# Two DMA queues, one for loads and one for stores, and uniform six-row chunks in a softmax with a relative-position bias

## The chip, the cores and the metric

The kernel runs on one core of a Trainium2 chip. The metric is device time in microseconds for one launch, the median of three runs. The work below is done by VectorE (DVE), ScalarE (ACT) and the 16 DMA engines; SyncE (SP) issues transfers, GpSimd (POOL) makes a few index numbers at the start, and TensorE isn't used.

## The reference

```
B, H, S = 2, 8, 2112          # logits (B, H, S, S) f32, rel_bias (H, 33) f32
rel  = pos[:, None] - pos[None, :]
bias = rel_bias[:, clip(rel, -16, 16) + 16]      # (H, S, S)
x = logits + bias
out = exp(x - x.max(-1)) / sum(exp(x - x.max(-1)))
```

Each of the 2 x 8 x 2112 = 33,792 rows of 2,112 numbers (8,448 bytes) gets a bias that depends on the column's distance from the diagonal alone, and then a softmax. The input and the output are 285.47 MB each.

## The kernel before

**Layout.** A partition holds W = 33 neighbouring rows of one head, so 64 partitions hold a head (64 x 33 = 2112) and 128 partitions hold two. A loop over K = 4 pairs of heads contains the two batch entries; each is cut into chunks of 6, 5, 6, 5, 6 and 5 rows a partition (SIZES). A round has NT = 12 chunks, and the whole kernel 48. Four buffers X (NBUF = 4) of 6 rows each take the chunks in turn.

**The bias.** Within one head, a partition's rows differ only in where the bias band lies. For every pair of heads, strip(k) (lines 143 to 158) builds one strip F of 2112 + 32 columns in SBUF, and row i of a chunk adds a window of F that starts one column further left per row. The masks eq, lt and gt of the strip lie in PSUM (Z). The bias table is fetched once by a DMA that ACT issues (line 107), and spread over partitions by a shuffle on DVE (line 134).

**A chunk's chain.** Line numbers are those of the profile.
- load (line 88): one DMA on SP's queue; 128 partitions, each a contiguous run of 5 or 6 rows.
- add on DVE (line 173): for each row one custom instruction, x + bias in place with the row's negated maximum as a by-product; semaphore `added`.
- exps on ACT (line 181): for each row exp in place, with the row's sum as a by-product; semaphore `expd`.
- scale on DVE: a reciprocal over the chunk's sums (line 189) once all rows are through, and the first DV = 3 rows multiplied by it (line 193). scale_rest on ACT: the other 2 or 3 rows (line 198). DVE and ACT take all this in program order, so the adds of a chunk come behind the scalings of the chunk before.
- store (line 96): one DMA, also on SP's queue, once the rows are scaled.

Waits on a semaphore are recorded under line 83, the helper take.

**SP's order.** SP is the only engine that issues these transfers, in an order written out by hand (turn, lines 210 to 214): store chunk n; wait until the store of chunk n-1 has landed; load chunk n+3 into the buffer that this has freed. Loads and stores so alternate in one queue. The last chunk is stored in two parts.

Of the kernel before, what the change touches and what calls it, by code (L numbers as in the profile page):

```python
# [15 lines left out]
def kernel(  # L16
# [14 lines left out]
    assert NB * W == S and 2 * NB == P and H % 2 == 0  # L31
    FW = S + W - 1
    BIG = 3.0e38
    NBUF = 4
    SIZES = [6, 5, 6, 5, 6, 5]
    R = max(SIZES)
    assert sum(SIZES) == W

    CH = [(b, sum(SIZES[:i]), r) for b in range(B) for i, r in enumerate(SIZES)]
    NT = len(CH)  # L40
    assert NT % NBUF == 0
# [4 lines left out]
    rbP = io.tile([P, H // 2, W], FP32, tag="rbP", name="rbP")  # L46
    rbK = io.tile([P, W], FP32, tag="rbK", name="rbK")
    rest = io.tile([P, NB], FP32, tag="rest", name="rest")
    nmax = io.tile([P, NBUF * R], FP32, tag="nmax", name="nmax")
    tot = io.tile([P, NBUF * R], FP32, tag="tot", name="tot")  # L50
    rec = io.tile([P, NBUF * R], FP32, tag="rec", name="rec")
    ps = ctx.enter_context(tc.tile_pool(name="ps", bufs=1, space=bass.MemoryType.PSUM))
    Z = ps.tile([P, 512], FP32, tag="Z", name="Z")
    eq, lt, gt = (Z[:, i * NB : (i + 1) * NB] for i in range(3))

    def view(t, offset, dims):
        return bass.AP(tensor=t.tensor, offset=t.offset + offset, ap=[[list(t.ap[0])[0], P]] + dims)

    def rows(t, k, m, s0, n):

        b, j, r = CH[m]
        return bass.AP(
            tensor=t.tensor,
            offset=t.offset + (b * H * S + j + s0) * S + k * (2 * S * S),
            ap=[[W * S, P], [1, n * S]],
        )

    with tc.tile_critical(no_gpsimd_drain=True):  # L68
# [5 lines left out]
        scaledA = nc.alloc_semaphore("scaledA")  # L74
        inv = nc.alloc_semaphore("inv")
        invA = nc.alloc_semaphore("invA")
# [5 lines left out]
        def take(eng, sem, n):  # L82
            eng.wait_ge(sem, n).then_inc(sem, -n)  # L83


        def load(k, m):
            b, r = m % NBUF, CH[m][2]
            nc.sync.dma_start(out=X[b][:, 0 : r * S], in_=rows(logits, k, m, 0, r)).then_inc(ld[b], 16)

        def store(k, m, s0=0, n=None):  # L90
            b, n = m % NBUF, n or CH[m][2]
# [4 lines left out]
            nc.sync.dma_start(  # L96
                out=rows(out, k, m, s0, n), in_=X[b][:, s0 * S : (s0 + n) * S]
            ).then_inc(st[b], 16)

        for m in range(NBUF):  # L100
            load(0, m)

        Q = 32
        step = list(F.ap[0])[0]
        nc.vector.memset(F[:, 0 : H * W], 0.0).then_inc(zero, 1)  # L105
        nc.scalar.wait_ge(zero, 1)
        nc.scalar.dma_start(
            out=bass.AP(tensor=F.tensor, offset=F.offset, ap=[[Q * step, P // Q], [1, H * W]]),
            in_=bass.AP(tensor=rel_bias.tensor, offset=rel_bias.offset, ap=[[0, P // Q], [1, H * W]]),
        ).then_inc(rb, 16)  # L110
        for p0 in (0, NB):
            nc.gpsimd.iota(  # L112
                F[p0 : p0 + NB, H * W : H * W + NB], pattern=[[-1, NB]], base=0,
                channel_multiplier=1, allow_small_or_imprecise_dtypes=True,
            ).then_inc(idx, 1)

        v = nc.vector
        done = [0]
# [11 lines left out]
        iq = F[:, H * W : H * W + NB]  # L130
        for m, op in ((eq, ALU.is_equal), (lt, ALU.is_gt), (gt, ALU.is_lt)):
            then(v.tensor_scalar(out=m, in0=iq, scalar1=0.0, scalar2=None, op0=op))  # L132
        v.wait_ge(rb, 16)
        then(v.stream_shuffle(out=F[:, 0 : H * W], in_=F[:, 0 : H * W], mask=[0] * Q))  # L134
        settle()
        for h in range(2):
            p = slice(h * NB, (h + 1) * NB)
            src = bass.AP(tensor=F.tensor, offset=F[p].offset + h * W,
                          ap=[[list(F.ap[0])[0], NB], [2 * W, K], [1, W]])
            then(v.tensor_copy(out=rbP[p], in_=src))  # L140
        settle()

        def strip(k):

            then(v.tensor_copy(out=rbK[:, :], in_=rbP[:, bass.ds(k, 1), :]))  # L145
            settle()
            low, high = rbK[:, W - 1 : W], rbK[:, 0:1]
            blocks = view(F, MR, [[W, NB], [1, W]])
            then(v.tensor_tensor(out=blocks, in0=view(eq, 0, [[1, NB], [0, W]]),  # L149
                                 in1=view(rbK, W - 1, [[0, NB], [-1, W]]), op=ALU.mult))  # L150
            then(v.tensor_scalar(out=rest, in0=lt, scalar1=low, scalar2=None, op0=ALU.mult))  # L151
            then(v.tensor_copy(out=F[:, 0:MR], in_=low.to_broadcast([P, MR])))  # L152
            then(v.tensor_copy(out=F[:, FW - MR : FW], in_=high.to_broadcast([P, MR])))  # L153
            settle()
            then(v.scalar_tensor_tensor(out=rest, in0=gt, scalar=high, in1=rest, op0=ALU.mult, op1=ALU.add))  # L155
            settle()
            then(v.tensor_tensor(out=blocks, in0=blocks, in1=view(rest, 0, [[1, NB], [0, W]]), op=ALU.add))  # L157
            settle()

        def row(m, i):  # L160
            return X[m % NBUF][:, i * S : (i + 1) * S]

        def col(t, m, i, n=1):
            c = m % NBUF * R + i
            return t[:, c : c + n]

        DV = 3

        def add(m):
            take(v, ld[m % NBUF], 16)  # L170
            j, r = CH[m][1:]
            for i in range(r):
                v.tensor_tensor_reduce(  # L173
                    out=row(m, i), in0=row(m, i), in1=F[:, W - 1 - j - i : W - 1 - j - i + S],
                    scale=-1.0, scalar=BIG, op0=ALU.add, op1=ALU.min, accum_out=col(nmax, m, i),
                ).then_inc(added, 1)

        def exps(m):
            for i in range(CH[m][2]):
                take(nc.scalar, added, 1)  # L180
                nc.scalar.activation(  # L181
                    out=row(m, i), in_=row(m, i), func=ACTF.Exp, scale=-1.0, bias=col(nmax, m, i),
                    accum_out=col(tot, m, i),
                ).then_inc(expd, 1)

        def scale(m):
            r = CH[m][2]
            take(v, expd, r)
            v.reciprocal(out=col(rec, m, 0, r), in_=col(tot, m, 0, r)).then_inc(inv, 1)  # L189
            v.wait_ge(inv, 1).then_inc(inv, -1)  # L190
            v.sem_inc(invA, 1)
            for i in range(DV):
                v.tensor_scalar_mul(out=row(m, i), in0=row(m, i), scalar1=col(rec, m, i)).then_inc(scaled, 1)  # L193

        def scale_rest(m):
            take(nc.scalar, invA, 1)
            for i in range(DV, CH[m][2]):
                nc.scalar.activation(  # L198
                    out=row(m, i), in_=row(m, i), func=ACTF.Copy, scale=col(rec, m, i),
                ).then_inc(scaledA, 1)  # L200
# [19 lines left out]
        store(0, 0)  # L220
        with nc.Fori(0, K - 1, 1, engines=[ENG.SP]) as k:
            turn(k, 1, NT + 1)
        turn(K - 1, 1, NT - 3)
        for m in range(NT - 3, NT - 1):
            store(K - 1, m)
        r = CH[NT - 1][2]
        store(K - 1, NT - 1, 0, DV)
        store(K - 1, NT - 1, DV, r - DV)
        for b in range(NBUF):
            take(nc.sync, st[b], 32 if b == (NT - 1) % NBUF else 16)  # L230


# [28 lines left out]
```

## Time and profile before

| | |
|---|---|
| median of 3 runs | 1330.0 us (1329.25 to 1330.1) |
| profiled execution | 1329.3 us, span 1327.5 us |
| DVE, ACT busy | 819.7 us, 808.8 us |
| add, 264 rows, mean of one | 2354 ns (and 82 ns to read the maximum) |
| exp, 264 rows, mean of one | 2054 ns (and 187 ns to read the sum) |
| scaling, DVE 144 rows, ACT 120 rows, mean of one | 1316 ns, 2046 ns |
| DMA | 13,981 packets, 571.00 MB, mean 430 GB/s |
| load, store of 6 rows, issue to landing (median) | 39.7 us, 46.9 us |

The span runs from the first to the last recorded event on the core; the execution's own time is 1.8 us longer. The time from issue to landing includes the wait behind other transfers in the queue. In the tables of the profile each row is a line of the kernel, an engine and an operation, with its count, total and mean time.

### The profile page before, as it was taken

Reading aid. Unit: us, or ns where it says so; the run is one execution under the profiler, and the core shown is the slowest. Engines: PE = TensorE matmul, PEld = TensorE weight load, DVE = VectorE, ACT = ScalarE, POOL = GpSimd, SP = SyncE. Lnnn points to the kernel's source line nnn. Section 1 sums busy time; section 2 is a strip of 40 time slices with the busy share of each in tenths; the row PEclk is TensorE's granted clock in tenths of the full one; section 3 lists DMA queues with packets and bytes.
Section 4 is the critical chain, followed back from the end, with each engine's and each line's share of the span. In section 5 each row is a group of like instructions: output and inputs, shape, how many; then the busy total and the mean of one; then the engine's idle time right before and its main releaser. Section 6 shows DMA issues by size and latency. Waiting matters only on the chain. (4 is left out here: it accounts for less than half of the span.)

```text
span 1327.5 us, 2383 instructions
## 1 busy us (share of the span) xinstructions
DVE 819.7 (62%) x756; ACT 808.8 (61%) x652; POOL 0.6 (0%) x6
## 2 busy tenths in 40 slices
DVE  6875665558655566556866466664686547665572
ACT  3885575655756557555676566764667646675472
POOL 0000000000000000000000000000000000000000
DMA  9999999999999999999999999999999999999998
GB/s 407 427 424 425 430 433 429 432 431 433 434 430 438 423 439 431 432 432 433 438 436 429 433 430 435 433 430 441 427 439 428 435 431 437 434 436 427 436 427 376
DMA packets 13981, 571.00 MB, mean 430 GB/s; under 512 B 1556, under 2 KB 1560, under 8 KB 1560
## 3 DMA queue, kind: packets, MB, share of 16 engines
q1 hardware_dynamic: 13968, 570.96, 99.8%
q14 instruction: 5, 0.04, 0.0%
q10 hardware_dynamic: 8, 0.00, 0.0%
HBM read 285.48 MB, written 285.47 MB: 430 GB/s over the span
## 5 line engine op out<-in xcount | busy, mean ns | idle before, releaser
L173 DVE CUSTOM_DVE_ANT_0 X<-X,F 128x2112 f32<-128x2112 f32 x264 | 605.5, 2354 | 346.8 <-DVEq L83 346.8
L181 ACT ACTIVATE X<-X,nmax 128x2112 f32<-128x2112 f32 x264 | 542.2, 2054 | 411.5 <-ACTq L83 385.7
L198 ACT ACTIVATE X<-X,rec 128x2112 f32<-128x2112 f32 x120 | 238.7, 2046 | 29.0 <-ACTq L83 29.0
L193 DVE TENSOR_SCALAR X<-X,rec 128x2112 f32<-128x2112 f32 x144 | 181.4, 1316 | 11.6 <-DVEq L190 11.6
L189 DVE RECIPROCAL rec<-tot 128x6 f32<-128x6 f32 (+1 forms) x48 | 9.1, 190 | 116.1 <-DVEq L83 116.1
L181 ACT ACTIVATION_READ_ACCUMULATOR X<-X,nmax 128x1 f32 x264 | 49.3, 187 | 0.0
L181 ACT ACT_TABLE_LOAD x4 | 5.1, 1283 | 55.8 <-ACTq L83 55.8
L173 DVE DVE_READ_ACCUMULATOR2_ANT nmax<- 128x1 f32 x264 | 21.7, 82 | 0.0
L157 DVE TENSOR_TENSOR F<-F,rest 128x2112 f32<-128x2112 f32 x4 | 9.4, 2358 | 0.6
L149 DVE TENSOR_TENSOR F<-Z,rbK 128x2112 f32<-128x2112 f32 x4 | 9.4, 2358 | 0.6
L134 DVE LOAD_MASK_SELECT F<-F x1 | 0.0, 14 | 7.1 <-DMA F<-in_rel_bias_dram 7.1
L155 DVE SCALAR_TENSOR_TENSOR rest<-Z,rbK,rest 128x64 f32<-128x64 f32 x4 | 1.1, 284 | 0.6 <-DVEq L83 0.2
L151 DVE TENSOR_SCALAR rest<-Z,rbK 128x64 f32<-128x64 f32 x4 | 1.1, 275 | 0.0
L105 DVE MEMSET F<- 128x264 f32 x1 | 0.3, 278 | 1.1 <-SPq L68 1.1
L145 DVE COPY rbK<-rbP 128x33 f32 x4 | 0.7, 178 | 0.3 <-DVEq L83 0.3
L153 DVE COPY F<-rbK 128x16 f32<-128x16 f32 x4 | 0.7, 168 | 0.0
L152 DVE COPY F<-rbK 128x16 f32<-128x16 f32 x4 | 0.7, 166 | 0.0
L132 DVE TENSOR_SCALAR Z<-F 128x64 f32<-128x64 f32 x3 | 0.5, 223 | 0.1
L140 DVE COPY rbP<-F 64x132 f32<-64x132 f32 x2 | 0.4, 224 | 0.2
L134 DVE STREAM_SHUFFLE F<-F 128x264 f32<-128x264 f32 x1 | 0.4, 443 | 0.0
L112 POOL IOTA F<- 64x64 f32 x2 | 0.4, 179 | 0.7 <-PEq L256 0.6
L245 POOL MEMSET const-bfloat16-1.0<- 128x1 bf16 x1 | 0.1, 103 | 0.0
(3 smaller groups left out, 0.3 us busy)
## 6 DMA issues: line engine op xcount, KB each, us to landing
X<-in_logits_dram SPq DMA_DIRECT2D x24, 6336.0 KB, 39.7
out_dram<-X SPq DMA_DIRECT2D x24, 6336.0 KB, 46.9
X<-in_logits_dram SPq DMA_DIRECT2D x24, 5280.0 KB, 42.2
out_dram<-X SPq DMA_DIRECT2D x23, 5280.0 KB, 48.6
out_dram<-X SPq DMA_DIRECT2D x1, 3168.0 KB, 16.5
out_dram<-X SPq DMA_DIRECT2D x1, 2112.0 KB, 21.1
F<-in_rel_bias_dram ACTq DMA_DIRECT2D x1, 4.1 KB
```

The lines of the kernel that those rows point to most:

```text
L145: then(v.tensor_copy(out=rbK[:, :], in_=rbP[:, bass.ds(k, 1), :]))
L149: then(v.tensor_tensor(out=blocks, in0=view(eq, 0, [[1, NB], [0, W]]), in1=view(rbK, W - 1, [[0, NB], [-1, W]]), op=ALU.mult))
L151: then(v.tensor_scalar(out=rest, in0=lt, scalar1=low, scalar2=None, op0=ALU.mult))
L152: then(v.tensor_copy(out=F[:, 0:MR], in_=low.to_broadcast([P, MR])))
L153: then(v.tensor_copy(out=F[:, FW - MR : FW], in_=high.to_broadcast([P, MR])))
L155: then(v.scalar_tensor_tensor(out=rest, in0=gt, scalar=high, in1=rest, op0=ALU.mult, op1=ALU.add))
L157: then(v.tensor_tensor(out=blocks, in0=blocks, in1=view(rest, 0, [[1, NB], [0, W]]), op=ALU.add))
L173: v.tensor_tensor_reduce(out=row(m, i), in0=row(m, i), in1=F[:, W - 1 - j - i : W - 1 - j - i + S], scale=-1.0, scalar=BIG, op0=ALU.add, o ...
L181: nc.scalar.activation(out=row(m, i), in_=row(m, i), func=ACTF.Exp, scale=-1.0, bias=col(nmax, m, i), accum_out=col(tot, m, i),).then_inc( ...
L189: v.reciprocal(out=col(rec, m, 0, r), in_=col(tot, m, 0, r)).then_inc(inv, 1)
L193: v.tensor_scalar_mul(out=row(m, i), in0=row(m, i), scalar1=col(rec, m, i)).then_inc(scaled, 1)
L198: nc.scalar.activation(out=row(m, i), in_=row(m, i), func=ACTF.Copy, scale=col(rec, m, i),).then_inc(scaledA, 1)
```

## The change

The rows are laid out anew. A partition now holds RP = 264 neighbouring rows, so that 8 partitions hold a head and the 128 partitions hold all 16 heads at once. A loop of K = 11 rounds goes over 24 rows a partition each (G = 4 buffers x 6 rows); every chunk has 6 rows and always the same buffer. There are 44 chunks.

The bias strip is built once, for all partitions, as F of 2112 + 263 = 2375 columns in PSUM. At the start of every round, window(k) copies the 2135 columns that the round's 24 rows need into F2 in SBUF, and the adds read F2.

Loads stay on SP's queue, each issued when the store of the same buffer has landed. Stores are issued by ACT on its own queue, after the scalings of the chunk, and wait for all six rows. DVE scales DV = 4 rows of a chunk and ACT two. The last chunk's store is no longer split. The semaphores scaled and scaledA become one, as do inv and invA.

```diff
-    NB = S // W
-    K = H // 2
-    FW = S + W - 1
+    RP = B * H * S // P
+    NB = S // RP
+    FW = S + RP - 1
-    SIZES = [6, 5, 6, 5, 6, 5]
-    CH = [(b, sum(SIZES[:i]), r) for b in range(B) for i, r in enumerate(SIZES)]
-    NT = len(CH)
+    R = 6
+    G = NBUF * R
+    K = RP // G
+    SW = S + G - 1
+    DV = 4
...
-    F = io.tile([P, FW], FP32, tag="F", name="F")
+    F2 = io.tile([P, SW + 1], FP32, tag="F2", name="F2")
...
+    F = ps.tile([P, 2560], FP32, tag="F", name="F")
...
-    def rows(t, k, m, s0, n):
-        b, j, r = CH[m]
-            offset=t.offset + (b * H * S + j + s0) * S + k * (2 * S * S),
-            ap=[[W * S, P], [1, n * S]],
+    def rows(t, k, m):
+            tensor=t.tensor, offset=t.offset + m * R * S + k * (G * S), ap=[[RP * S, P], [1, R * S]],
...
-        def store(k, m, s0=0, n=None):
-            if s0 < DV:
-                take(nc.sync, scaled, DV)
-            if s0 + n > DV:
-                take(nc.sync, scaledA, s0 + n - DV)
-            nc.sync.dma_start(
-                out=rows(out, k, m, s0, n), in_=X[b][:, s0 * S : (s0 + n) * S]
-            ).then_inc(st[b], 16)
+        def store(k, m):
+            take(nc.scalar, scaled, R)
+            nc.scalar.dma_start(out=rows(out, k, m), in_=X[m][:, :]).then_inc(st[m], 16)
 
         for m in range(NBUF):
             load(0, m)
+        with nc.Fori(0, K - 1, 1, engines=[ENG.SP]) as k:
+            for m in range(NBUF):
+                take(nc.sync, st[m], 16)
+                load(k + 1, m)
+        for m in range(NBUF):
+            take(nc.sync, st[m], 16)
...
+        C0 = RP - 1 - MR
+        bands = view(F, C0, [[RP, NB], [1, W]])
+        then(v.tensor_tensor(out=bands, in0=view(eq, 0, [[1, NB], [0, W]]), in1=view(rbK, W - 1, [[0, NB], [-1, W]]),
+                             op=ALU.mult))
+        then(v.tensor_tensor(out=bands, in0=bands, in1=view(rest, 0, [[1, NB], [0, W]]), op=ALU.add))
+        then(v.tensor_copy(out=view(F, C0 + W, [[RP, NB - 1], [1, RP - W]]),
+                           in_=view(reg, 1, [[1, NB - 1], [0, RP - W]])))
...
+        def window(k):
+            then(v.tensor_copy(out=F2[:, 0:SW], in_=F[:, bass.ds(RP - G - k * G, SW)]))
             settle()
...
         with nc.Fori(0, K, 1, engines=[ENG.DVE]) as k:
-            strip(k)
-            for m in range(NT):
+            window(k)
+            for m in range(NBUF):
                 add(m)
                 scale(m)
-        with nc.Fori(0, K, 1, engines=[ENG.Activation]):
-            for m in range(NT):
+        with nc.Fori(0, K, 1, engines=[ENG.Activation]) as k:
+            for m in range(NBUF):
                 exps(m)
                 scale_rest(m)
-        def turn(k, first, stop):
-            for n in range(first, stop):
-                store(k + n // NT, n % NT)
-                take(nc.sync, st[(n - 1) % NBUF], 16)
-                load(k + (n + 3) // NT, (n + 3) % NT)
...
-        store(K - 1, NT - 1, 0, DV)
-        store(K - 1, NT - 1, DV, r - DV)
+                store(k, m)
```

More of the change, by code (lines that the diff above doesn't have):

```diff
@@ L126, in settle @@
             done[0] = 0
-        v.wait_ge(idx, 2)
-        iq = F[:, H * W : H * W + NB]
-        for m, op in ((eq, ALU.is_equal), (lt, ALU.is_gt), (gt, ALU.is_lt)):
-            then(v.tensor_scalar(out=m, in0=iq, scalar1=0.0, scalar2=None, op0=op))
+        Q = 32
+        step = list(F2.ap[0])[0]
+        T = F2[:, 0 : H * W]
+        v.memset(T, 0.0).then_inc(zero, 1)
+        nc.scalar.wait_ge(zero, 1)
+        nc.scalar.dma_start(
+            out=bass.AP(tensor=F2.tensor, offset=F2.offset, ap=[[Q * step, P // Q], [1, H * W]]),
+            in_=bass.AP(tensor=rel_bias.tensor, offset=rel_bias.offset, ap=[[0, P // Q], [1, H * W]]),
+        ).then_inc(rb, 16)
@@ new lines @@
+        nc.gpsimd.iota(pid[:, :], pattern=[[0, 2]], base=0, channel_multiplier=1).then_inc(idx, 1)
+        nc.gpsimd.iota(
+            num, pattern=[[1, NB + 1]], base=0, channel_multiplier=0,
+            allow_small_or_imprecise_dtypes=True,
+        ).then_inc(idx, 1)
+        v.wait_ge(idx, 2)
+        then(v.tensor_scalar(out=pid[:, 0:1], in0=pid[:, 0:1], scalar1=NB - 1, scalar2=None, op0=ALU.bitwise_and))
+        then(v.tensor_scalar(out=pid[:, 1:2], in0=pid[:, 1:2], scalar1=3, scalar2=H - 1,
+                             op0=ALU.logical_shift_right, op1=ALU.bitwise_and))
@@ L133 @@
+        settle()
+        then(v.tensor_copy(out=qh, in_=pid[:, :]))
+        settle()
+        q, h = qh[:, 0:1], qh[:, 1:2]
+        for o, n, s, op in ((eq, NB, q, ALU.is_equal), (lt, NB, q, ALU.is_lt), (hsel, NB, h, ALU.is_equal),
+                            (le, NB + 1, q, ALU.is_le), (gt, NB + 1, q, ALU.is_gt)):
+            then(v.tensor_scalar(out=o, in0=num[:, 0:n], scalar1=s, scalar2=None, op0=op))
         v.wait_ge(rb, 16)
-        then(v.stream_shuffle(out=F[:, 0 : H * W], in_=F[:, 0 : H * W], mask=[0] * Q))
+        then(v.stream_shuffle(out=T, in_=T, mask=[0] * Q))
@@ L135 @@
         settle()
[L136 to L140, printed above, removed]
-        settle()
[L143 to L157, printed above, removed]
@@ new lines @@
+        heads = view(F2, H * W, [[W, H], [1, W]])
+        then(v.tensor_tensor(out=heads, in0=view(F2, 0, [[W, H], [1, W]]), in1=view(hsel, 0, [[1, H], [0, W]]),
+                             op=ALU.mult))
+        settle()
+        then(v.tensor_reduce(out=rbK, in_=view(F2, H * W, [[1, W], [W, H]]), axis=mybir.AxisListType.X, op=ALU.add))
+        settle()
+        low, high = rbK[:, W - 1 : W], rbK[:, 0:1]
+        C0 = RP - 1 - MR
+        bands = view(F, C0, [[RP, NB], [1, W]])
+        then(v.tensor_scalar(out=rest, in0=lt, scalar1=low, scalar2=None, op0=ALU.mult))
@@ new lines @@
+        then(v.tensor_scalar(out=reg, in0=le, scalar1=low, scalar2=None, op0=ALU.mult))
+        settle()
+        then(v.scalar_tensor_tensor(out=rest, in0=gt[:, 0:NB], scalar=high, in1=rest, op0=ALU.mult, op1=ALU.add))
+        then(v.scalar_tensor_tensor(out=reg, in0=gt, scalar=high, in1=reg, op0=ALU.mult, op1=ALU.add))
+        then(v.tensor_tensor(out=bands, in0=view(eq, 0, [[1, NB], [0, W]]), in1=view(rbK, W - 1, [[0, NB], [-1, W]]),
+                             op=ALU.mult))
+        settle()
@@ L158, in strip @@
             settle()
         def row(m, i):
-            return X[m % NBUF][:, i * S : (i + 1) * S]
+            return X[m][:, i * S : (i + 1) * S]
         def col(t, m, i, n=1):
-            c = m % NBUF * R + i
+            c = m * R + i
             return t[:, c : c + n]
-        DV = 3
         def add(m):
-            take(v, ld[m % NBUF], 16)
-            j, r = CH[m][1:]
-            for i in range(r):
+            take(v, ld[m], 16)
+            for i in range(R):
+                x = G - 1 - m * R - i
@@ L178, in exps @@
         def exps(m):
-            for i in range(CH[m][2]):
-                take(nc.scalar, added, 1)
+            for i in range(R):
+                if i < R - 1:
+                    nc.scalar.wait_ge(added, i + 1)
+                else:
+                    take(nc.scalar, added, R)
                 nc.scalar.activation(
@@ L184, in exps, with scales_begin @@
                 ).then_inc(expd, 1)
-        def scale(m):
[L187 to L191, printed above, removed]
+        def scales_begin(eng, m):
+            if m < NBUF - 1:
+                eng.wait_ge(inv, m + 1)
+            else:
+                take(eng, inv, NBUF)
+        def scale(m):
+            take(v, expd, R)
+            v.reciprocal(out=col(rec, m, 0, R), in_=col(tot, m, 0, R)).then_inc(inv, 1 if m < NBUF - 1 else NBUF + 1)
+            scales_begin(v, m)
             for i in range(DV):
@@ L195, in scale_rest @@
         def scale_rest(m):
-            take(nc.scalar, invA, 1)
-            for i in range(DV, CH[m][2]):
+            scales_begin(nc.scalar, m)
+            for i in range(DV, R):
                 nc.scalar.activation(
                     out=row(m, i), in_=row(m, i), func=ACTF.Copy, scale=col(rec, m, i),
-                ).then_inc(scaledA, 1)
+                ).then_inc(scaled, 1)
         with nc.Fori(0, K, 1, engines=[ENG.DVE]) as k:
-            strip(k)
-            for m in range(NT):
+            window(k)
+            for m in range(NBUF):
                 add(m)
                 scale(m)
-        with nc.Fori(0, K, 1, engines=[ENG.Activation]):
-            for m in range(NT):
+        with nc.Fori(0, K, 1, engines=[ENG.Activation]) as k:
+            for m in range(NBUF):
                 exps(m)
                 scale_rest(m)
-        def turn(k, first, stop):
-            for n in range(first, stop):
-                store(k + n // NT, n % NT)
-                take(nc.sync, st[(n - 1) % NBUF], 16)
-                load(k + (n + 3) // NT, (n + 3) % NT)
[L220 to L226, printed above, removed]
-        store(K - 1, NT - 1, 0, DV)
-        store(K - 1, NT - 1, DV, r - DV)
-        for b in range(NBUF):
-            take(nc.sync, st[b], 32 if b == (NT - 1) % NBUF else 16)
+                store(k, m)
 _INS = ['logits', 'rel_bias']
```

47 lines of the change are left out of this document (19 added, 28 removed).

## The prediction, made before the changed kernel was run

> **What bounds the kernel now.** I read the page of the profile first: the span, the busy shares, the DMA slices and queues.
>
> ```profile
> span 1327.5 us, 2383 instructions
> DVE 819.7 (62%) x756; ACT 808.8 (61%) x652; POOL 0.6 (0%) x6
> ...
> DMA packets 13981, 571.00 MB, mean 430 GB/s; under 512 B 1556, under 2 KB 1560, under 8 KB 1560
> ...
> q1 hardware_dynamic: 13968, 570.96, 99.8%
> q14 instruction: 5, 0.04, 0.0%
> q10 hardware_dynamic: 8, 0.00, 0.0%
> ```
>
> No compute engine is busy for two thirds of the time, while queue q1 (SP's, with every load and store) keeps the 16 DMA engines at 99.8% of the span. ACT's own queue q10 carries eight packets in all. Then I cut the span into stretches (columns: length, busy us of DVE, ACT and POOL, clock, DMA share, GB/s).
>
> ```profile
> 0.00:100.00 100.00, 73.29 (x75) 67.90 (x55) 0.56 (x6) 1.00 1.00 421
> 100.00:300.00 200.00, 118.92 (x107) 119.56 (x96) 0.00 (x0) 1.00 1.00 429
> 300.00:500.00 200.00, 127.73 (x118) 122.38 (x99) 0.00 (x0) 1.00 1.00 433
> 500.00:700.00 200.00, 128.14 (x121) 127.50 (x105) 0.00 (x0) 1.00 1.00 434
> 700.00:900.00 200.00, 118.40 (x107) 120.92 (x97) 0.00 (x0) 1.00 1.00 432
> 900.00:1100.00 200.00, 125.93 (x116) 119.06 (x97) 0.00 (x0) 1.00 1.00 434
> 1100.00:1300.00 200.00, 123.29 (x112) 127.03 (x103) 0.00 (x0) 1.00 1.00 432
> 1300.00:1327.50 27.50, 3.97 (x4) 4.41 (x4) 0.00 (x0) 1.00 0.85 366
> ```
>
> From 100 to 1300 us the share is 1.00 and the rate (429+433+434+432+434+432)/6 = 432.3 GB/s: the engines are never without a packet. Only the ends are below that. The waits say the same from the other side: the long waits of DVE and ACT are for data.
>
> ```profile
> ACT X L181 <- ACTq L83: 385.7, 44, 12.5
> DVE X L173 <- DVEq L83: 346.8, 45, 10.3
> ```
>
> So the kernel is bound by moving 571.0 MB through 16 busy engines; 571.0/0.4323 = 1320.8 us of the 1327.5 are the bytes at the middle rate. The other 6.7 us are the start and the drain. A change can gain those 6.7 us and no more, unless it alters the rate itself; it loses whenever it leaves the engines idle or slows a packet.
>
> **The bytes.** Every logit is still read once and written once: 88 transfers of 128 partitions x 6 rows x 8,448 B = 6.488 MB are the same 570.95 MB. Transfers fall from 97 (48 loads, 49 stores) to 88, and a transfer grows from 5 or 6 rows to 6. Since both sizes already run back to back at a share of 1.00, I price this at nothing, in either direction under a microsecond. At 432.3 GB/s one transfer alone takes 15.0 us; a load and a store together, sharing the engines, 30.0 us; 44 such pairs 1320.6 us.
>
> **Compute under the new order.** A chunk's chain can be read from the first chunk of before:
>
> ```profile
> 18.60 2.36 DVE L173 CUSTOM_DVE_ANT_0 X<-X,F 128x2112 f32<-128x2112 f32 x1 [2.15 <-DVEq L83]
> ...
> 34.87 0.19 DVE L189 RECIPROCAL rec<-tot 128x6 f32<-128x6 f32 x1 [2.50 <-DVEq L83]
> 35.30 3.78 DVE L193 TENSOR_SCALAR X<-X,rec 128x2112 f32<-128x2112 f32 x3 [0.24 <-DVEq L190]
> 35.33 5.95 ACT L198 ACTIVATE X<-X,rec 128x2112 f32<-128x2112 f32 x3 [0.61 <-ACTq L83]
> ...
> 41.38 16.61 SPq L96 DMA_DIRECT2D out_dram<-X  x2
> ```
>
> From the first add to the first scaling is 35.30 - 18.60 = 16.7 us and is unchanged. Then DVE scales four rows instead of three (3.78/3 = 1.26 each, 5.04 us) beside ACT's two (5.95/3 = 1.98 each, 3.97 us). So a chunk ends 21.7 us after its first add, where it took until 41.38 (22.8 us) before, and DVE may begin the next one there. 44 x 21.7 = 955 us, and the window copies come on top.
>
> The window copy (2,135 columns from PSUM to SBUF, once a round) is not in the trace. Its nearest rows are a one-input operation and a two-input one of nearly the same width:
>
> ```profile
> L193 DVE TENSOR_SCALAR X<-X,rec 128x2112 f32<-128x2112 f32 x144 | 181.4, 1316 | 11.6 <-DVEq L190 11.6
> L157 DVE TENSOR_TENSOR F<-F,rest 128x2112 f32<-128x2112 f32 x4 | 9.4, 2358 | 0.6
> ```
>
> So 1.3 to 2.4 us, eleven times: 14 to 26 us. I take the upper end, since its source lies in PSUM. Of the four strips that go, the second full-width operation alone took 9.4 us (row L157). Total 955 + 26 = 981 us against 1320.6 us of transfers: 8 us a chunk of slack covers the copies. If that cover were gone, they would cost their 26 us.
>
> **The store moves to ACT.** ACT waits until all six rows are scaled (5.04 - 3.97 = 1.1 us for DVE), then issues the transfer. Queued behind it on ACT are the next chunk's exponentials, which need the next first add, 2.4 us after DVE's last scaling. An issue on ACT in before and one on SP:
>
> ```profile
> 1.39 1.10 ACTq L107 DMA_DIRECT2D F<-in_rel_bias_dram  x1
> 1250.08 56.24 SPq L96 DMA_DIRECT2D out_dram<-X  x4
> ```
>
> The ACT row is 1.10 us, so it fits under the 2.4 us: nothing. SP then waits for nothing but store m's landing before load m of the next round; four buffers last 4 x 30 = 120 us against 30 (load) + 21.7 + 30 (store) = 82 us in use, so 38 us of queueing keep both queues fed.
>
> **Start.**
>
> ```profile
> 0.97 1.88 SPq L88 DMA_DIRECT2D X<-in_logits_dram  x4
> ...
> 9.08 0.44 DVE L134 STREAM_SHUFFLE F<-F 128x264 f32<-128x264 f32 x1
> ...
> 14.10 2.36 DVE L157 TENSOR_TENSOR F<-F,rest 128x2112 f32<-128x2112 f32 x1
> ```
>
> The bias table has landed at 9.08 us in before, its strip is ready at 14.10 + 2.36 = 16.46, and the first add starts at 18.60. The new setup makes one 2,375-wide band after the same landing and then the window: more small operations, one fill of 1,617 columns and one copy in place of the second full-width operation. I put its end at 18 to 25 us. Even 25 gives the first store by 25 + 21.7 = 47 us, when the four loads (60 us from 2 us on) still occupy the engines: nothing.
>
> **End.** This is the only term I find. The first store comes at about 41.4 us, when 62 - 41.4 = 20.6 us of loads are left. If the two queues share equally from there, load 3 lands at 41.4 + 41.2 = 82.6 and load n+3 at 82.6 + 30n: load 43 at 1282.6 us. Store n ends at 71.4 + 30n; store 41 would end at 1301.4, but has the engines alone from 1282.6 on and ends at 1292.0, store 42 at 1307.0. Chunk 43 is scaled and issued at 1282.6 + 21.7 + 1 = 1305.3 us: 1.7 us to spare. But the engines do not finish together. From the timeline of before the first add of its last chunk, and from its stretches the drain:
>
> ```profile
> 1286.66 2.36 DVE L173 CUSTOM_DVE_ANT_0 X<-X,F 128x2112 f32<-128x2112 f32 x1 [7.08 <-DVEq L83]
> ...
> 1322.00:1324.00 2.00, 0.00 (x0) 0.00 (x0) 0.00 (x0) 1.00 0.61 262
> 1324.00:1326.00 2.00, 0.00 (x0) 0.00 (x0) 0.00 (x0) 1.00 0.20 84
> ```
>
> The share falls over 4 us in before's drain, so a landing is that of the slowest engine, up to 4 us late while other engines may already have run dry. In place of 1.7 us to spare there is 0 to 3 us of idle; I take 1.5. Before has no such gap: its last chunk starts at 1286.66 with stores still queued (the row of four issues from 1250.08 on).
>
> How two queues share an engine isn't in this trace: q10 was idle. I take equal shares, between two ends: loads first (then the last chunk is early and the gap is 0) and stores first (a rival, below). The Trainium skill (DMA: Bandwidth & Descriptors, "Queues, rings and completion order") says that each engine takes turns between the queues that have work, a packet at a time; by it the sum would be the one just made.
>
> **Sum.** 1327.5 + 1.5 = 1329.0 us of span. The profiled run took 1329.3 with a span of 1327.5, so 1.8 us lie around it: 1330.8. The profiled run is 0.7 us under the median of 1330.0: 1331.5 us, 0.1% slower, which is less than the 0.2% (2.7 us) that a measurement of this kernel can tell from no change. With an idle of 0 to 3 us, and 1.5 us either way for the ends, this case alone spans 1328.5 to 1334.5.
>
> **Rivals.**
> - Mixed traffic is slower. Before sends all engines one load, then one store; now each engine alternates. Against: between 500 and 1300 us before switches direction every 12 to 15 us and holds 432 to 434 GB/s. For: the first 300 us, when the first stores begin, show 421 and 429. At 429 throughout the middle 1,200 us grow by 0.8%, 9 us: 1341. At 421 the whole takes 571.0/0.421 = 1356 us, 1358 with what lies around. It decides from a loss of 0.2% a packet on.
> - Stores go first, or the last load is late for another cause. Then only a store or nothing lies behind the last load, and most of chunk 43's 21.7 us is bare: about +20, 1350 us. Against: nothing gives one queue a preference here.
> - Faster: the two queues fill each other's gaps at the start and the drain, or read and write partly overlap. The gaps are 6.7 us, so at best 1323 if the middle holds; at the best 200-us rate throughout, 571.0/0.434 = 1315.7, 1318 with what lies around. Against: a share of 1.00 leaves no gap in the middle.
> - The addresses. Partitions were 33 rows apart (278,784 B), now 264 rows (2,230,272 B), so the simultaneous streams could meet in the memory. At the lowest rate that a 10-us stretch of before shows, the row below, 571.0/0.405 = 1410 us. For it nothing in this trace speaks, as all of before has the narrow spacing.
>
> ```profile
> 80.00:90.00 10.00, 8.79 (x8) 9.47 (x9) 0.00 (x0) 1.00 0.97 405
> ```
>
> The Trainium skill (DMA: Bandwidth & Descriptors, "Latency and other measured facts") speaks against the change here: it has copies falling from 207 to 164 GB/s a direction as the spacing of partitions goes from 512 KiB to 2 MiB, and back to 214 when a 4 MiB spacing is padded by 4 KiB. No run here shows it yet; the new spacing is 2 MiB and 130 KiB, so by its remedy the rate would hold.
>
> **How the numbers follow.** Forecast 0.50 (0.36 within 0.2%, 0.10 above, 0.04 below); mixed traffic 0.22 (0.02 within, else slower); bare last chunk 0.08; faster 0.14; addresses 0.06. So faster 0.18, same 0.38, slower 0.44. The likeliest case gives 1331.5. The range runs from 1325 (leaving out most of the faster case, 0.10) to 1350 (leaving out the addresses and the worse of mixed traffic, 0.10).
>
> **What would show it.** Right: q1 and q10 near half of the packets' time each, their sum near 100%; stretches from 100 to 1280 us at a share of 1.00 and 430 to 434 GB/s; the last load landing near 1283 us and the last store issued by ACT near 1306, with a dip of the share just before it; DVE and ACT waiting 8 us a chunk for data. Wrong: a middle rate off 432 GB/s by over 2 either way (mixed traffic, overlap, addresses), or a hole of over 5 us in the DMA near the end.

## The result and the profile after

The changed kernel takes 1326.37 us (median of 19 runs, 1325.38 to 1336.22) against 1329.54 us of the kernel before (19 runs, 1328.61 to 1330.29): a ratio of 0.998, interval 0.9971 to 0.9989. It is 3.2 us faster (0.2%, which a measurement of this kernel can just tell), where the forecast was 1.5 us slower. Of the 19 runs 17 lie below 1328, one at 1329.2 and one at 1336.2; the experiments come back to such long runs.

The profiled execution took 1327.36 us with a span of 1325.6. From its page:

```profile
span 1325.6 us, 2109 instructions
DVE 866.1 (65%) x781; ACT 757.2 (57%) x627; POOL 0.4 (0%) x6
...
DMA packets 12682, 570.98 MB, mean 431 GB/s; under 512 B 1412, under 2 KB 1416, under 8 KB 1416
...
q1 hardware_dynamic: 6336, 285.48, 50.1%
q10 hardware_dynamic: 6344, 285.48, 49.8%
...
L170 DVE COPY F<-F 128x2135 f32 x11 | 26.1, 2373 | 0.5 <-DVEq L86 0.5
```

The two queues share the engines' time by halves, and together still fill 99.9% of it. The same stretches as before (length, busy us of DVE, ACT and POOL, clock, DMA share, GB/s):

```profile
0.00:100.00 100.00, 79.57 (x86) 63.64 (x54) 0.43 (x6) 1.00 0.99 422
100.00:300.00 200.00, 128.07 (x112) 111.24 (x92) 0.00 (x0) 1.00 1.00 430
300.00:500.00 200.00, 132.77 (x119) 118.66 (x99) 0.00 (x0) 1.00 1.00 433
500.00:700.00 200.00, 129.82 (x115) 113.81 (x96) 0.00 (x0) 1.00 1.00 433
700.00:900.00 200.00, 127.75 (x112) 111.39 (x91) 0.00 (x0) 1.00 1.00 434
900.00:1100.00 200.00, 133.10 (x119) 118.98 (x100) 0.00 (x0) 1.00 1.00 432
1100.00:1300.00 200.00, 129.82 (x115) 114.94 (x96) 0.00 (x0) 1.00 1.00 433
1300.00:1325.60 25.60, 5.20 (x5) 4.56 (x4) 0.00 (x0) 1.00 0.86 374
```

The middle moves (430+433+433+434+432+433)/6 = 432.5 GB/s, before 432.3: neither mixing loads and stores on an engine nor the wide spacing shows in the middle rate. The end, from the timeline and from stretches of 5 us:

```profile
1284.53 2.36 DVE L184 CUSTOM_DVE_ANT_0 X<-X,F 128x2112 f32<-128x2112 f32 x1 [8.49 <-DVEq L86]
...
1306.28 0.34 ACTq L93 DMA_DIRECT2D out_dram<-X  x1
...
1300.00:1305.00 5.00, 4.15 (x5) 4.54 (x4) 0.00 (x0) 1.00 1.05 456
1305.00:1310.00 5.00, 1.05 (x1) 0.01 (x1) 0.00 (x0) 1.00 1.08 466
1310.00:1315.00 5.00, 0.00 (x0) 0.00 (x0) 0.00 (x0) 1.00 0.91 395
1315.00:1320.00 5.00, 0.00 (x0) 0.00 (x0) 0.00 (x0) 1.00 0.98 426
1320.00:1325.00 5.00, 0.00 (x0) 0.00 (x0) 0.00 (x0) 1.00 0.40 172
1325.00:1331.00 6.00, 0.00 (x0) 0.00 (x0) 0.00 (x0) 1.00 0.00 0
```

The last chunk's first add starts at 1284.53 and its store is issued at 1306.28; there is no hole around it (a hole is a stretch near the end in which engines have nothing to do). (A packet counts in the stretch in which it starts, so a share can pass 1.00.) The drain is where the two kernels differ. The same stretches of the kernel before have their last two at 0.67 and 0.02:

```profile
1320.00:1325.00 5.00, 0.00 (x0) 0.00 (x0) 0.00 (x0) 1.00 0.67 289
1325.00:1331.00 6.00, 0.00 (x0) 0.00 (x0) 0.00 (x0) 1.00 0.02 8
```

Since the two kernels' last packets differ in size, the packet records themselves tell it better. Put together from the trace, packet by packet (us; a packet is called slow by what it takes beyond the median of its size, 1.872 for 50,688 B and 1.561 for 42,240 B; "per engine" sums this up over the run). The records don't name the engine of a packet: packets are joined to 16 chains in which each starts where the one before ends, with 8 packets and a semaphore write to a transfer, so what is said of a single engine is less certain than the means. "Changed, again" is a second profile of the changed kernel, of a run at 1325.67 us:

```
                       sum of medians   slow time per engine    last data of an engine
                       per engine       mean   least   most     first to end   last to end
before                 1318.3           5.4    3.7     7.5      1321.9         1326.1
changed                1317.9           4.8    3.8     5.8      1322.1         1324.0
changed, again         1317.9           2.0    1.5     4.1      1319.5         1322.3
changed, one queue     1317.9           4.1    1.5     11.1     1322.4         1329.3
```

In the first three the 16 engines work without a pause to the end; with one queue the early ones wait some 2.5 us near 1305. Of the 2.1 us by which the last engine ends earlier (1326.1 to 1324.0), 0.4 are fewer packets, 0.6 fewer slow packets on average, and 1.1 that the last engine is closer to the mean. In the second profile the last engine ends 3.8 us earlier than before, and there 3.4 are fewer slow packets, 0.4 fewer packets, and nothing is a closer end: the last engine is some 2.2 us behind the mean, as in the kernel before. Its stretches from 100 to 1300 us all move 434 GB/s. Its run is the more usual kind, since 15 of the changed kernel's 27 runs lie at 1325.4 to 1325.9. So the gain is, by these profiles, for the most part time that slow packets no longer take. Slow packets are mostly loads: in the changed kernel's traces no store packet of 50,688 B takes over 1.91 us, while the slowest loads take 3.1 and 3.3. Stores count on one engine all the same: in both traces the engine that ends last has some 100 stores slow by 0.01 to 0.03 us each, 1.8 us in all.

### The profile page after: what moved, and what is told of

Its sections match the earlier page's. It is cut to its first block, busy times and chain, and to the rows that moved or that the text cites. A ratio compares the mean times of both kernels' runs of the same rounds, so it can differ in the third digit from the quotient of the medians.

```text
span 1325.6 us, 2109 instructions
## 1 busy us (share of the span) xinstructions
DVE 866.1 (65%) x781; ACT 757.2 (57%) x627; POOL 0.4 (0%) x6
## 3 DMA queue, kind: packets, MB, share of 16 engines
q1 hardware_dynamic: 6336, 285.48, 50.1%
q10 hardware_dynamic: 6344, 285.48, 49.8%
## 5 line engine op out<-in xcount | busy, mean ns | idle before, releaser
L184 DVE CUSTOM_DVE_ANT_0 X<-X,F 128x2112 f32<-128x2112 f32 x264 | 605.2, 2354 | 322.3 <-DVEq L86 322.3
L211 DVE TENSOR_SCALAR X<-X,rec 128x2112 f32<-128x2112 f32 x176 | 220.3, 1315 | 2.8
L216 ACT ACTIVATE X<-X,rec 128x2112 f32<-128x2112 f32 x88 | 176.1, 2048 | 17.2 <-DVE rec L208 12.2
L208 DVE RECIPROCAL rec<-tot 128x6 f32<-128x6 f32 x44 | 8.4, 191 | 106.2 <-DVEq L86 106.2
L170 DVE COPY F<-F 128x2135 f32 x11 | 26.1, 2373 | 0.5 <-DVEq L86 0.5
L184 DVE DVE_READ_ACCUMULATOR2_ANT nmax<- 128x1 f32 x264 | 21.7, 82 | 0.0
```

The source lines that it names most:

```text
L170: then(v.tensor_copy(out=F2[:, 0:SW], in_=F[:, bass.ds(RP - G - k * G, SW)]))
L184: v.tensor_tensor_reduce(out=row(m, i), in0=row(m, i), in1=F2[:, x : x + S], scale=-1.0, scalar=BIG, op0=ALU.add, op1=ALU.min, accum_out=c ...
L208: v.reciprocal(out=col(rec, m, 0, R), in_=col(tot, m, 0, R)).then_inc(inv, 1 if m < NBUF - 1 else NBUF + 1)
L216: nc.scalar.activation(out=row(m, i), in_=row(m, i), func=ACTF.Copy, scale=col(rec, m, i),).then_inc(scaled, 1)
```

## The experiments

Two theories stood against each other at first: that the gain comes from the two queues (Q), and that it comes from the new rows and the equal, fewer transfers (L).

**One queue.** The changed kernel, with its stores on SP in the order of before.

```diff
-            take(nc.scalar, scaled, R)
-            nc.scalar.dma_start(out=rows(out, k, m), in_=X[m][:, :]).then_inc(st[m], 16)
+            take(nc.sync, scaled, R)
+            nc.sync.dma_start(out=rows(out, k, m), in_=X[m][:, :]).then_inc(st[m], 16)
...
+            for n in range(1, NBUF + 1):
+                store(k + n // NBUF, n % NBUF)
+                take(nc.sync, st[n - 1], 16)
+                load(k + 1, n - 1)
```

> The changed kernel with its stores back on SP's queue, in the order of before (store n, wait for store n-1, load n+3); rows, chunks, strip and scaling as changed. Theory Q (the 3.2 us gained come from the two queues: the DMA engines run less far apart): it falls back, to about 1328.5 to 1329.5, with the engines ending some 4 us apart. Rival L (the gain comes from the new rows and the fewer, equal transfers, on whatever queue): it stays at 1326 to 1327.

Measured: 1331.59 us (11 runs, 1329.3 to 1333.6), 1.0013 of before (1.0004 to 1.0022). It loses the whole gain and 2 us more than Q had said, so the new rows gain nothing on one queue, and L falls. Its 200-us stretches from 100 to 1300 us move 432 to 434 GB/s, as in the other two; the loss is a few engines that end late, seen in the drain:

```profile
1315.00:1320.00 5.00, 0.00 (x0) 0.00 (x0) 0.00 (x0) 1.00 0.84 365
1320.00:1325.00 5.00, 0.00 (x0) 0.00 (x0) 0.00 (x0) 1.00 0.56 243
1325.00:1331.00 6.00, 0.00 (x0) 0.00 (x0) 0.00 (x0) 1.00 0.08 34
```

In the packet records the mean slow time is 4.1 us an engine, less than the 4.8 of the first profile of the changed kernel. But eleven engines have 2.1 us or less, the other five 6.0 to 11.1, and these five end last: on the worst, one packet is slow by 0.1 to 0.9 us in most loads from 108 to 713 us, mostly at steps of 30 us. The end is set by the worst engine.

**The old rows on two queues.** The kernel before, with its stores issued by ACT and SP left with loads.

```diff
+                store(k, m)                       # ACT, after scale_rest(m)
...
+                take(nc.sync, st[n % NBUF], 16)
+                load(k + (n + 4) // NT, (n + 4) % NT)
```

> The kernel before (33 rows a partition, chunks of 6 and 5 rows) with its stores issued by ACT on its own queue, the last chunk's in one piece, and SP issuing loads alone. Theory Q: it gains what the change gained but for the fewer packets (0.4 us), about 1326.5 to 1327.5. Rival L: it stays at 1329 to 1330.

Measured: 1337.86 us (5 runs, 1335.91 to 1338.75), 1.0059 (1.0045 to 1.0072). Neither theory: two queues alone cost 8 us here. Its packet records have 10.4 us of slow packets an engine, and its profile has what the changed kernel's lacks, a hole before the last store:

```profile
1300.00:1310.00 10.00, 9.84 (x9) 6.96 (x7) 0.00 (x0) 1.00 1.04 449
1310.00:1320.00 10.00, 5.61 (x6) 7.78 (x6) 0.00 (x0) 1.00 0.63 273
1320.00:1330.00 10.00, 0.00 (x0) 0.00 (x0) 0.00 (x0) 1.00 0.96 415
```

**Sizes or spacing.** Two runs to tell what about the old rows does it. One keeps the changed kernel and takes 22 rows a round, in chunks of 6, 5, 6 and 5; the other changes the addresses alone.

```diff
-            tensor=t.tensor, offset=t.offset + m * R * S + k * (G * S), ap=[[RP * S, P], [1, R * S]],
+            tensor=t.tensor, offset=t.offset + m * R * S + k * (P * G * S), ap=[[G * S, P], [1, R * S]],
```

> The changed kernel with 22 rows a round in chunks of 6, 5, 6 and 5 rows (12 rounds, 48 chunks as in before); 264 rows a partition and two queues as changed. Theory Z (the old rows on two queues were slow because transfers of unequal size let loads and stores slip past each other on an engine): it becomes slow too, 1333 to 1338. Rival N (it was the 33-row spacing of the partitions): it stays at 1326.5 to 1328, 0.4 us of packets above the changed kernel.

> The changed kernel with only the addresses changed: partitions 24 rows apart in place of 264 (a round takes 3,072 neighbouring rows). Every row is still read and written once, but the bias band that is added is that of another row, so the output isn't the reference's. Theory Z: the spacing doesn't matter, 1326 to 1327.5. Rival N: loads become slow as with the old rows, 1333 to 1338.

Measured: the unequal sizes 1328.23 us (10 runs: five at 1326.4 to 1327.8, four at 1328.6 to 1333.7, one at 1338.1; 0.9994, 0.9981 to 1.0007), the narrow spacing 1332.5 us (12 runs: three at 1325.7 to 1327.2, three at 1328 to 1330.1, six at 1335 to 1337.1; 1.0012, 0.9993 to 1.0031). Both theories fall: runs at 1333 to 1338 come with either edit, and with neither always. What changes is how often a run is long. These runs had no changed kernel beside them on the same chip; for the narrow spacing the comparison on one chip comes below, for the unequal sizes there is none. The one profile with unequal sizes (1338.08 us) lost 4.5 of its 7.6 us of slow packets an engine after 1200 us, and its stores were slow too, up to 2.65 us. The profile of the narrow version is of a long run, and shows the hole again, with the last chunk 7.9 us later than in the changed kernel (its first add at 1292.38):

```profile
1292.38 2.36 DVE L184 CUSTOM_DVE_ANT_0 X<-X,F 128x2112 f32<-128x2112 f32 x1 [8.49 <-DVEq L86]
...
1290.00:1300.00 10.00, 7.62 (x7) 4.96 (x5) 0.00 (x0) 1.00 1.05 456
1300.00:1310.00 10.00, 7.44 (x8) 9.06 (x9) 0.00 (x0) 1.00 0.55 238
1310.00:1320.00 10.00, 3.90 (x4) 2.87 (x2) 0.00 (x0) 1.00 0.67 289
```

**One queue at the narrow spacing.**

> The same narrow addresses with all stores on SP's queue in the order of before (bias bands misplaced as in the run above). If one queue lets a few engines collect the slow load packets whatever the spacing (theory Q): 1329 to 1333. If it was the wide spacing that made the changed rows slow on one queue (1331.6 against 1329.7 of before): 1328 to 1329.5.

Measured: 1330.78 us (11 runs, 1328.37 to 1332.4), 1.0004 (0.9995 to 1.0013), with the engines ending between 1320.6 and 1327.5 us in the profile. This is theory Q again, and the wide spacing is not what made one queue slow. On one queue no run at either spacing is above 1333.6, and none is below 1328.4.

**Twice the transfers.** Eight buffers of 3 rows.

```diff
-    NBUF = 4
-    R = 6
+    NBUF = 8
+    R = 3
-    DV = 4
+    DV = 2
```

> The changed kernel with eight buffers of 3 rows in place of four of 6, DVE scaling two of three rows: 176 transfers in place of 88, the same bytes. In the trace of before a packet of half the size took 0.940 us and one of the full size 1.872. Theory: a packet costs 4 ns beyond its bytes and a transfer 9 ns an engine, so 1,408 x 4 ns + 88 x 9 ns = 6.4 us more, 1332 to 1334. Rival C (all of the 3.2 us came from the nine transfers that went, 0.35 us each): 88 x 0.35 = 31 us more, 1357.

Measured: 1331.28 us (10 runs, 1330.05 to 1331.69), 4.9 us above the changed kernel, against the 6.4 of the working and the 31 of the rival. The sum of the packets' medians in its trace is 5.6 us higher (1323.5 against 1317.9). So the transfers that the change took out are worth 0.4 us, as the table has it, and not the 3.2.

**A later chunk.** ACT scales all six rows (DV = 0), or four (DV = 2).

> The changed kernel with all six rows of a chunk scaled by ACT (DVE none), so that a chunk is ready some 6.9 us later (11.9 us of ACT copies in place of 5.0 us of DVE). ACT then needs 26 us a chunk, still under the 30 us of its transfers. Theory E (the changed kernel's last store comes with about 1 us to spare before the engines run dry, and whatever is later is paid in full): about 6 us more, 1331 to 1333, with a hole in the DMA at 1308 to 1314 us. Rival (the queues hold more backlog than the prediction's end term says): no change, 1326 to 1327.

> The changed kernel with DVE scaling two rows of a chunk and ACT four: a chunk is ready 2.9 us later (7.9 us of ACT copies in place of 5.0 us of DVE). Theory E (what the last chunk is late beyond about 1 us of margin is paid one for one): 1328 to 1329.5. Rival (the lateness also lets stores slip against loads, as in most timed runs of the version that was 6.9 us later): 1331 or more, with a wide scatter.

Measured: all six 1339.79 us (5 runs: one at 1332.09, four at 1339.6 to 1342.8; 1.0089, 1.0074 to 1.0105); four 1326.88 us (12 runs: seven at 1325.9 to 1327, one at 1331.2, four at 1336.2 to 1337.8; 0.9997, 0.9977 to 1.0017). The profiled run of the first is the one at 1332.09. There the packet records show the engines waiting 5.1 to 6.7 us from 1307.1 to 1308.6 us on, as theory E has it. The other four runs lose a further 7.5 to 10.7 us. In the second version theory E fails: seven of 12 runs are no slower than the changed kernel, where it said 1328 to 1329.5. No such short run was profiled, so why 2.9 us a chunk can cost nothing is open. The profiled run of the second is a long one:

```profile
1293.94 2.36 DVE L184 CUSTOM_DVE_ANT_0 X<-X,F 128x2112 f32<-128x2112 f32 x1 [10.96 <-DVEq L86]
...
1300.00:1310.00 10.00, 7.71 (x8) 9.36 (x10) 0.00 (x0) 1.00 0.63 274
1310.00:1320.00 10.00, 2.74 (x3) 7.89 (x4) 0.00 (x0) 1.00 0.25 106
```

Its last chunk starts 9.4 us later than in the changed kernel; most engines have nothing to do from 1306 to 1309 us on, for 10 to 14 us. In its packet records one engine has 14.5 us of slow loads where the median engine has 3.7, and a store's landing differs between the first and the last engine by 2 us at the start and 23 us near the end. In the kernel a load waits for the store of its buffer on all engines, and the trace shows what that does. Store 39 has landed on 15 engines by 1237.7 us and on the last one at 1256.0; SP issues load 43, the last one, behind it at 1256.6 (the second issue of the row below), where the changed kernel issues it at 1245.95:

```profile
1245.95 0.33 SPq L89 DMA_DIRECT2D X<-in_logits_dram  x1
...
1226.68 30.22 SPq L89 DMA_DIRECT2D X<-in_logits_dram  x2
```

The first row is the changed kernel's, the second this run's. So the last load lands at 1289.1 to 1293.4 us (in the changed kernel at 1281.9 to 1284.0), the last chunk is late for all engines, and those that aren't behind have worked off the other stores by then. The long runs of the narrow version and of the shortest and longest hold (below) look the same: SP issues load 43 at 1255.0 to 1255.7, behind one to three engines that have 11 us or more of slow packets.

**The last chunk in pairs.** If the hole is what a long run costs, it can be filled: in the last chunk alone each pair of rows is scaled as soon as its sums are there, and SP stores it.

```diff
+        for p in range(3):
+            take(nc.sync, scaled2 if p < 2 else scaled3, 2)
+            nc.sync.dma_start(
...
+                in_=X[Lm][:, 2 * p * S : (2 * p + 2) * S],
+            ).then_inc(st[Lm], 16)
```

> The changed kernel whose last chunk alone is finished in three pairs of rows: each pair is scaled as soon as its exponentials are done, and SP, whose queue has no loads left, stores it; the first pair leaves some 12 us after the chunk's first add in place of 21.7. Theory H (two queues end in one of two ways: the last load lands near 1284 us and the last store comes in time, 1326 us, or it lands some 10 us later, the engines run dry and the time is 1336): the second ending is filled, every run 1325 to 1328, median 1325.5 to 1326.5. Rival (the 10 us are lost during the run, in slow packets): as the changed kernel, with a rare run at 1336.

> The version whose chunks are ready 2.9 us later (DVE scales two rows, ACT four; 5 of its 12 runs lay at 1331 to 1338), with the last chunk finished in pairs. Theory H: all runs 1325 to 1328. Rival: still some four in ten at 1336.

> The version with partitions 24 rows apart on two queues (bias bands misplaced; 6 of its 12 runs lay at 1335 to 1337, 6 at 1326 to 1330), with the last chunk finished in pairs. Theory H: the upper group is gone, all runs 1325 to 1330. Rival: half the runs stay at 1335 to 1337.

> The changed kernel itself, beside the three above on the same chip, so that single runs can be compared. By its 19 runs so far: 1325.4 to 1327.5 for nearly all, and at most one or two of some twelve near 1336.

Measured: in pairs 1325.86 us (11 runs, 1325.6 to 1330.03; 0.9977, 0.9968 to 0.9985), the changed kernel beside it 1325.8 us (8 runs, 1325.67 to 1327.1; 0.9974, 0.9964 to 0.9984): no difference, so this isn't a better version. With chunks 2.9 us later, 1327.46 us, three of 12 runs still at 1335 to 1337; narrow, 1330.03 us, four of 12 still at 1334 to 1337. These were timed on one chip: two kernels without a run above 1330.1 in 19, and beside them the later chunks and the narrow spacing, which bring long runs there too. Theory H half falls. In the narrow version's profile, again of a long run, the pairs go out from 1305.14 us on, and the engines' pauses, mostly 8 to 10 us in the narrow version before, shrink to under 4:

```profile
1305.14 9.80 SPq L292 DMA_DIRECT2D out_dram<-X  x3
...
1310.00:1315.00 5.00, 3.66 (x4) 3.92 (x3) 0.00 (x0) 1.00 0.65 277
1315.00:1320.00 5.00, 0.00 (x0) 0.00 (x0) 0.00 (x0) 1.00 1.02 433
```

But the engine that is behind ends at 1332.0 all the same, when most others have ended at about 1323.5. The hole was the form in which its delay reached the others; the delay itself stays.

**The first store held.** Open was whether the start decides which run is long. Here ACT holds the first store until the next chunk's first, second or sixth add. For this the first round stands outside of ACT's loop.

```diff
+                if m == 0:
+                    nc.scalar.wait_ge(added, 1)    # or 2, or 6; first round alone
                 store(0, m)
```

> The changed kernel, in which ACT holds the first store alone until the next chunk's first add is done: it leaves 2.4 us later, about when it leaves in the version that was 2.9 us late a chunk; all that follows is as changed. Theory I (whether an engine stays behind for the whole run is decided in the first 100 us, by where the first stores meet the loads): runs near 1331 to 1338 appear, some 3 or more of 12, where the changed kernel had 1 of 27. Rival P (it was the later chunks all through the run): as the changed kernel, 1325.5 to 1327.5.

> The same with the second add: the first store leaves 4.7 us later. Theory I: another share of slow runs than above, with no order in the delays needed, since the place within a packet of 1.9 us counts. Rival P: 1325.5 to 1327.5.

> The same with the sixth add: the first store leaves 13.8 us later, near 54 us, when the fourth load is under way; DVE's and ACT's work is not held up. Theory I: another share of slow runs. Rival P: 1325.5 to 1327.5. By the prediction's term for the end the loads get a lead of some 7 us more here, so a gap at the end is less likely than in the changed kernel.

Measured: held to the first add 1329.97 us (12 runs: three to 1327.7, six at 1328.5 to 1331.6, three at 1335.6 to 1337.9; 1.0005, 0.9989 to 1.0021); to the second 1332.12 us (9 runs, none under 1331.2; 1.0026, 1.0016 to 1.0036); to the sixth 1336.01 us (12 runs: one at 1325.6, three at 1329.9 to 1332.1, eight at 1335.8 to 1336.9; 1.0032, 1.0017 to 1.0047). In the profiles the first store moves from 40.34 us to 42.42, 44.67 and 53.85. With the longest hold the hole is there:

```profile
53.85 0.38 ACTq L93 DMA_DIRECT2D out_dram<-X  x1
...
1300.00:1310.00 10.00, 7.43 (x10) 9.00 (x9) 0.00 (x0) 1.00 0.57 248
1310.00:1320.00 10.00, 4.62 (x4) 3.60 (x2) 0.00 (x0) 1.00 0.59 253
```

Only the shortest hold moves one store alone. ACT takes its work in order, so the next exponentials wait with the held store: with the longest hold the next three stores leave 10.5, 10.1 and 7.9 us later too (72.09 us for 61.64, 93.42 for 83.31, 114.87 for 106.93), against what its expectation says, and with the middle one the second store 1.3 us later. So a first store 2.1 us later goes with a median 3.6 us above the changed kernel's 1326.37, and the longer holds, which move more, with 6 and 10 us. The prediction's lead of the loads keeps no gap away. Two things were not tried beside them: the changed kernel on this chip, and the first round outside of the loop without a hold (in the profiles this also leaves one ACT_TABLE_LOAD on ACT in place of eleven). The rise from hold to hold is free of both.

Theory I holds in that the start changes how often a run is long; that it settles a single run was not seen. On the first 100 us the three profiles differ. With the shortest and the longest hold the worst engine's slow packets lie mostly at 400 to 1250 us (12.7 of 15.0 us and 11.6 of 15.5). With the middle one 6.3 of the 7.9 us of slow packets an engine lie in the first 100 us, on every engine, with stores slow up to 3.2 us. So long runs come about in more than one way. Why an engine's packets get slow is open; what the engines meet in, the traces don't show.

## Why the prediction was right or wrong

- **The bytes and the rate: right.** 432.5 against 432.3 GB/s (434 in the second profile, by fewer slow packets), and a share of 1.00 throughout. The rivals of mixed traffic and of addresses fall. The Trainium skill (DMA: Bandwidth & Descriptors, "Latency and other measured facts") has spacings of 2 to 8 MiB, powers of two, costing up to half of the rate, and a few KiB of padding restoring it; at 2 MiB and 130 KiB the rate held, as its remedy says.
- **Compute, window copy, the store on ACT: right.** 2373 ns a copy (taken: up to 2.4 us). The first store left at 40.34 us, 21.7 us after the first add at 18.66, and DVE waits 322.3 us for loads in 42 pieces, 7.7 each (said: 8):

```profile
DVE X L184 <- DVEq L86: 322.3, 42, 8.9
...
18.66 2.36 DVE L184 CUSTOM_DVE_ANT_0 X<-X,F 128x2112 f32<-128x2112 f32 x1 [0.94 <-DVEq L86]
...
40.34 0.38 ACTq L93 DMA_DIRECT2D out_dram<-X  x1
```

- **Equal shares of two queues: right.** Said: load 43 lands at 1282.6 and its store is issued at 1305.3; measured: the load lands at 1281.9 to 1284.0, depending on the engine, the first add is at 1284.53 and the issue at 1306.28. The Trainium skill (DMA: Bandwidth & Descriptors, "Queues, rings and completion order") has the engine take turns by packets; the two shares of 50.1% and 49.8% agree.
- **The end: the step that failed.** "In place of 1.7 us to spare there is 0 to 3 us of idle; I take 1.5" was 0: the engines finished the stores before the last one between 1306.8 and 1309.0, just as it came. And the sum added that 1.5 to a drain taken over from before unchanged, its "4 us" of engines ending apart included. That was the term of the sum that was mis-sized: the last engine ended 2.1 us earlier in the first profile, 4.1 us apart became 1.8, and 3.8 us earlier in the second. The prediction saw this spread as something of the drain alone; it is the sum of slow packets, mostly loads, over the whole run, different for each engine, 5.4 us in the mean of before and 4.8 and 2.0 here, and so something that an order of transfers can change. Of the 5.1 us between 1331.5 and the measured median, 1.5 are the idle that didn't come, 3.2 the gain, and 0.5 that the kernel before has a median of 1329.54 over 19 runs, not 1330.0.
- **The packets: priced at nothing, worth 0.4 us.**
- **The rival with the bare last chunk** was given 0.08 and "+20, 1350 us". It is real, at +10: one of the 27 runs of the changed kernel (1336.22) lies where the long runs of its variants do. No profile of that run exists, so that it has the same hole is inferred. In the long runs that were profiled the cause is not a preference for stores, the rival's first reason, but its second, a last load that is late; in the four followed above, it is late because engines fall behind.
- **Faster** was given 0.18, 0.14 of it for gaps that two queues fill at both ends or for an overlap of reads and writes. It came true for neither reason: in the records of before no engine pauses until its end, and the median packet of 50,688 B takes 1.872 us in both kernels. The gain was time of slow packets, a part of the middle rate that the prediction took as given. No run shows why they are fewer.

## What to carry to other kernels

When the DMA engines are busy throughout, the time is that of the slowest of the 16, and a mean rate or share doesn't show it: look at how far apart the engines end, and at how many runs of a kernel lie apart from the rest. Loads and stores on queues of their own gave engines that end within 2 to 3 us in the profiles of this kernel, and engines some 9 to 12 us behind the others in four profiled long runs of its variants, so such a gain of 0.2% can hang on things that nobody meant to change, the time of the first store or the addresses, and a kernel that gets it should be timed in many runs. A buffer's reload that waits for all 16 engines passes one engine's delay on to the others, and at the end it comes out as a hole. To fill the hole is not enough: the last chunk in pairs did so, and the engine behind still set the end.

## What the runs showed of the hardware that was not expected

- Load packets of 50,688 B took 1.872 us, or up to 3.1 and 3.3 in the changed kernel's two traces; store packets never over 1.91 there, but up to 2.1 to 3.2 in the profiled long runs of its variants. Slow packets cost an engine 1.5 to 11 us in the runs of the table, and up to 16 in the long run with chunks 2.9 us later.
- On one queue at the wide spacing five engines had 8 to 20 loads slow by over 0.15 us after the first 100 us, and the other eleven one at most.
- In the second profile of the changed kernel no load on any engine was slow by over 0.15 us after the first 100 us, where 1.8 of the 2.0 us of slow packets an engine lie, while the first profile has 119 such loads later, about 7 on every engine.
